# Seven block products in place of eight in 12 of 22 feed-forward pairs

## The chip, the cores and the metric

The kernel runs on one core of a Trainium2 chip. The metric is the device time of one execution in microseconds; several runs are given by their median.

## What is computed

Two layers act on 528 tokens (16 learned ones and a sequence of 512; the second layer hands out only the 512) of width 1024. A layer has four mixers that run side by side (a gated linear attention, a retention, a state-space branch, a gated delta rule), a gated sum of them, and a feed forward of hidden width 2816. The change is in the feed forward:

```python
    x = x + merged @ w_out
    h2 = rmsnorm(x, norm_ffn)
    gt, up = jnp.split(h2 @ w_gu, 2, axis=-1)
    return x + (jax.nn.silu(gt) * up) @ w_down
```

Everything is float32. The kernel reaches that precision on TensorE by splitting each operand into a high part (a cast to float32r) and a low part (the rest, value minus high part) and adding three products: high x high, high x low, low x high.

## The kernel before

Activations lie transposed, 128 channels on the partitions and the tokens in the free dimension. A weight panel of 128 output channels is 128 x 1024: eight blocks of 128 x 128, one for each k-block of the 1024 input channels. `wload` (line 180) brings a panel in two parts of four blocks: a DMA on SyncE's queue (L189, tile `wr`, 3 buffers), a cast on ScalarE to the high part (L190, tile `wh`, 5 buffers), a subtraction on VectorE for the low part (L192, tile `wl`, 5 buffers). `mmk` (L206) issues, for one k-block, the three products for each segment of tokens; `mm` does a panel, k-block by k-block, into one PSUM tile `pm` of two banks (2 buffers). Layer 0 has two segments of 264 tokens; layer 1 works on 512 tokens as one segment.

The 22 hidden panels of a feed forward come in three groups of 8, 7 and 7 (`FFG`). A pair is one gate panel and one up panel, of 128 hidden channels: two `mm` calls on the normalised activations `hh` and `hl`, then `silu2` (tanh on ScalarE, L365; (th + 1) x gate on VectorE, L366), the product with the up panel on VectorE (L1584), and the split of the result into `ah` and `al` (L199, L200). The factor of one half in the SiLU is put in afterwards. After each group `residual` multiplies the group's results by `w_down`, eight panels of 128 output channels, and adds to the residual stream `xs` on VectorE (L1545; the last two panels of the last group by halves of the tokens, L1555). The first pair of a layer goes by `head`, by halves of the tokens and mixed with the normalisation (`norm_sum`, `norm_finish`), whose own split is L199 and L200 on `hh` and `hl`.

The program orders TensorE's instructions by hand (`manual_schedule`); the other engines' order is set by the framework's scheduler, except that `after(ins)` puts the instructions traced within it behind `ins` on its engine. Side jobs are Python generators: `start` adds one, `pump` runs each by one step, `need` pumps until they are done. `mm` pumps once in four k-blocks.

One side job is `s5_prep` (line 1160): tables and matrices for the state-space branch, made from parameters alone, with many small VectorE operations (L1171), small matmuls (L1338), transposes (L1347) and DMAs to DRAM on GpSimd's and ScalarE's queues. Layer 0's runs beside the mixers of layer 0; layer 1's is started at the third pair of layer 0's feed forward and is needed at its end.

## Time and profile before

| | us |
|---|---|
| median of 3 runs | 2224.28 (2223.33 to 2229.99) |
| the profiled execution | 2226.7 |
| its span, first to last instruction | 2224.9 |
| TensorE busy | 2202.2 |
| VectorE busy | 1269.9 |
| ScalarE busy | 893.7 |

The span holds layer 0's mixers (to about 720 us), its feed forward (to about 1140), layer 1's mixers (to about 1835) and its feed forward (to about 2215). In the rows PE is TensorE's matmuls and PEld its weight loads, which run beside them; DVE is VectorE, ACT ScalarE, POOL GpSimd, SP SyncE. A matmul's duration runs from its start to its modelled end and overlaps the next one's, so the cost of one is the step from start to start. PEclk is the granted clock of TensorE as a share of 2.4 GHz.

### The profile page before, as it was taken

Reading aid. Unit: us, or ns where it says so; the run is one execution under the profiler, and the core shown is the slowest. Engines: PE = TensorE matmul, PEld = TensorE weight load, DVE = VectorE, ACT = ScalarE, POOL = GpSimd, SP = SyncE. Lnnn points to the kernel's source line nnn. Section 1 sums busy time; section 2 is a strip of 40 time slices with the busy share of each in tenths; the row PEclk is TensorE's granted clock in tenths of the full one; section 3 lists DMA queues with packets and bytes.
Section 4 is the critical chain, followed back from the end, with each engine's and each line's share of the span. In section 5 each row is a group of like instructions: output and inputs, shape, how many; then the busy total and the mean of one; then the engine's idle time right before and its main releaser. Section 6 shows DMA issues by size and latency. Waiting matters only on the chain. (4 is left out here: it accounts for less than half of the span.)

```text
span 2224.9 us, 41086 instructions
## 1 busy us (share of the span) xinstructions
PE 2202.2 (99%) x16300; PEld 2019.0 (91%) x16300; DVE 1269.9 (57%) x2505; ACT 893.7 (40%) x1920; POOL 189.5 (9%) x243
## 2 busy tenths in 40 slices
PE   9999999999999999999999999999999999999998
PEld 8999999999999999999999988787888888888887
DVE  7884566758444677533367844745385445434344
ACT  5653544433333433322346534644333334323232
POOL 2420021110000100000014121000000001000000
PEclk9999999999999999999999999999999999999999
DMA  4332222374233234332232332222643332332322
GB/s 129 104 105 66 86 77 77 111 228 141 89 91 119 96 110 124 124 87 94 88 119 83 106 95 83 75 72 72 202 122 90 95 123 91 90 100 91 98 93 83
DMA packets 144540, 229.73 MB, mean 103 GB/s; under 512 B 30044, under 2 KB 46884, under 8 KB 143836
## 3 DMA queue, kind: packets, MB, share of 16 engines
q1 hardware_dynamic: 136572, 208.98, 30.5%
q0 software_dynamic: 4032, 11.70, 1.6%
q10 hardware_dynamic: 3744, 6.42, 0.8%
q8 instruction: 128, 2.10, 0.4%
q14 instruction: 64, 0.52, 0.1%
HBM read 207.40 MB, written 19.65 MB: 102 GB/s over the span
## 5 line engine op out<-in xcount | busy, mean ns | idle before, releaser
L190 ACT CAST wh<-wr 128x512 fp32r<-128x512 f32 (+1 forms) x680 | 416.7, 614 | 1019.7 <-PE pm L206 841.7
L206 PE MATMUL pm<-hh,wh 128*128 128x264 f32 (+1 forms) x3120 | 799.6, 315 | 3.0 <-ACT hh L199 1.6
L206 PE MATMUL pm<-hl,wh 128*128 128x264 f32 (+1 forms) x3120 | 787.4, 312 | 5.6 <-POOL hl L200 2.9
L206 PE MATMUL pm<-hh,wl 128*128 128x264 f32 (+1 forms) x3120 | 783.2, 310 | 0.0
L192 DVE TENSOR_TENSOR wl<-wr,wh 128x512 fp32r<-128x512 f32 (+1 forms) x664 | 460.1, 695 | 537.3 <-ACT wh L190 528.3
L206 PEld LDWEIGHTS pm<-hh,wh 128*128 128x128 f32 x3120 | 513.5, 189 | 40.2 <-ACT hh L199 2.6
L206 PEld LDWEIGHTS pm<-hl,wh 128*128 128x128 f32 x3120 | 513.1, 189 | 38.9 <-POOL hl L200 4.4
L206 PEld LDWEIGHTS pm<-hh,wl 128*128 128x128 f32 x3120 | 512.8, 189 | 30.7
L206 PE MATMUL pm<-ah,wh 128*128 128x264 f32 (+2 forms) x542 | 146.0, 318 | 0.0
L206 PE MATMUL pm<-al,wh 128*128 128x264 f32 (+2 forms) x542 | 145.6, 317 | 0.0
L206 PE MATMUL pm<-ah,wl 128*128 128x264 f32 (+2 forms) x542 | 145.5, 317 | 0.0
L206 PE MATMUL pm<-bh,wh 128*128 128x264 f32 (+1 forms) x384 | 105.4, 328 | 0.8 <-DVE mg L445 0.5
L206 PE MATMUL pm<-bh,wl 128*128 128x264 f32 (+1 forms) x384 | 102.4, 321 | 0.0
L206 PE MATMUL pm<-bl,wh 128*128 128x264 f32 (+1 forms) x384 | 102.2, 320 | 0.0
L270 POOL TENSOR_TENSOR rs<-rs,mhalf 88x3 f32<-88x3 f32 (+1 forms) x10 | 8.4, 841 | 1060.1 <-ACT rs L269 1055.1
L206 PEld LDWEIGHTS pm<-ah,wh 128*128 128x128 f32 x542 | 91.4, 188 | 7.7 <-ACT wh L190 0.4
L206 PEld LDWEIGHTS pm<-al,wh 128*128 128x128 f32 x542 | 91.1, 188 | 7.2
L206 PEld LDWEIGHTS pm<-ah,wl 128*128 128x128 f32 x542 | 91.2, 188 | 6.9
L802 DVE SCALAR_TENSOR_TENSOR acc<-cvr,pk,acc 128x528 f32<-128x528 f32 x72 | 69.0, 960 | 8.8 <-ACT acc L799 7.9
L206 PEld LDWEIGHTS pm<-bh,wh 128*128 128x128 f32 x384 | 63.5, 188 | 8.1 <-DVE mg L445 1.3
L206 PEld LDWEIGHTS pm<-bh,wl 128*128 128x128 f32 x384 | 63.7, 188 | 5.4
L445 DVE SCALAR_TENSOR_TENSOR th<-th,pm 128x528 f32<-128x528 f32 (+1 forms) x48 | 33.3, 694 | 61.6 <-PE pm L206 55.4
(409 smaller groups left out, 2484.6 us busy)
## 6 DMA issues: line engine op xcount, KB each, us to landing
wr<-in_w_in SPq DMA_DIRECT2D x304, 256.0 KB, 2.7
wr<-in_w_gu SPq DMA_DIRECT2D x176, 256.0 KB, 2.6
wr<-in_w_br SPq DMA_DIRECT2D x64, 256.0 KB, 2.6
wr<-in_w_dn SPq DMA_DIRECT2D x64, 256.0 KB, 2.6
wr<-in_w_out SPq DMA_DIRECT2D x32, 256.0 KB, 2.6
wr<-in_w_dn SPq DMA_DIRECT2D x32, 192.0 KB, 2.4
s5mi<-s5m ACTq DMA_DIRECT2D x16, 256.0 KB, 3.1
mi<-s5mi SPq DMA_DIRECT2D x16, 256.0 KB, 3.7
```

Source lines behind the costliest of these rows:

```text
L190: i = nc.scalar.copy(hi[:, :n], raw[:, :n])
L192: j = eng.tensor_tensor(out=lo[:, :n], in0=raw[:, :n], in1=hi[:, :n].bitcast(F32), op=ALU.subtract)
L206: self.nc.tensor.matmul(ps[:m, i, :n], wt, x[k][:, t0:t0 + n], start=(k == 0 and i2 == 0), stop=(k == kt - 1 and i2 == 2))
L270: nc.gpsimd.tensor_tensor(out=dst, in0=dst, in1=self.mhalf[:dst.shape[0], :n], op=ALU.pow)
L445: nc.vector.scalar_tensor_tensor(out=self.sv(th, segs), in0=self.sv(th, segs), scalar=1.0, in1=br, op0=ALU.add, op1=ALU.mult)
L802: nc.vector.scalar_tensor_tensor(out=acc, in0=raw[:, w:w + T], scalar=conv[:, jt + w:jt + w + 1], in1=acc, op0=ALU.mult, op1=ALU.add)
```

## The change

In 12 pairs of each layer (`SEVEN`: the panels 4, 5, 7, 8, 10, 11, 13, 14, 16, 17, 19, 20) the two panels, the two halves of the 1024 input channels and the two halves of the tokens are seen as a product of 2 x 2 blocks and done with seven block products (Strassen's method in Winograd's form) in place of eight. `pair7` is such a pair. A product is 4 k-blocks x 3 terms = 12 matmuls over half of the tokens (264 in layer 0, 256 in layer 1). Three of its seven weight operands are panel halves as loaded, the other four (`s1` to `s4`) are sums and differences of such halves, made on VectorE (`comb`); each is then split as before. Three of the right-hand operands are blocks of `hh`, `hl` themselves, the other four are sums `T` of them, which `right_sums` makes once a layer beside pairs 1 to 3. Products add up in three PSUM tiles: `a` takes products 1, 3, 5 and 7 and is copied out on ScalarE after 1, 3 and 5 (`keep`); `c` takes 2 and 6, `d` takes 4. The four result blocks are put together in SBUF with `add`, and `finish` makes the SiLU product from them, in part by halves of the tokens.

The other pairs (`pair8`) keep their eight products, written as four units. `units` issues a list of units: the operands of a unit are traced four units before its products, behind the evictions of the three units before. `s5_prep` of layer 1 is started in layer 1's mixers, at the same place as layer 0's.

```diff
--- before.py
+++ after.py
@@ -54,6 +54,7 @@
     _o += _w
 NPK = _o
 FFG = [(0, 8), (8, 7), (15, 7)]
+SEVEN = [j for j in range(4, KF) if j % 3]
 
 
 def halves(segs):
@@ -1494,6 +1495,169 @@
         return bh, bl
 
 
+
+
+
+    def right_sums(self, segs):
+        nc = self.nc
+        (a0, n), (b0, _) = halves(segs)
+        t0 = a0
+        self.T = {}
+        rows = [self.f4(F32R, "xsum") for _ in range(2)]
+        for k in range(4):
+            top, low = self.f(name="xk"), self.f(name="xk")
+            for dst, kk in ((top, k), (low, k + 4)):
+                nc.vector.tensor_tensor(out=dst[:, t0:], in0=self.hh[kk][:, t0:].bitcast(F32),
+                                        in1=self.hl[kk][:, t0:].bitcast(F32), op=ALU.add)
+            b11, b12, b21, b22 = (x[:, c:c + n] for x in (top, low) for c in (a0, b0))
+            yield
+            for i in range(2):
+                t = self.f(name="xt")
+                x, y = t[:, 0:n], t[:, n:2 * n]
+                if i == 0:
+                    nc.vector.tensor_tensor(out=x, in0=b12, in1=b11, op=ALU.subtract)
+                    nc.vector.tensor_tensor(out=y, in0=b22, in1=x, op=ALU.subtract)
+                    nc.vector.tensor_tensor(out=b21, in0=b21, in1=y, op=ALU.subtract)
+                    sums = (1, 2)
+                else:
+                    nc.vector.tensor_tensor(out=x, in0=b22, in1=b12, op=ALU.subtract)
+                    nc.scalar.copy(y, b21)
+                    sums = (3, 4)
+                if i == 0:
+                    hi, lo = self.b(name="xsh"), self.b(name="xsl")
+                else:
+                    hi, lo = (r[:, k, :] for r in rows)
+                self.split(hi[:, :2 * n], lo[:, :2 * n], t[:, :2 * n])
+                for j, c in zip(sums, (0, n)):
+                    self.T[j, k] = (hi[:, c:c + n], lo[:, c:c + n])
+                yield
+
+    def pair7(self, srcs, segs, finish):
+        nc = self.nc
+        hs = halves(segs)
+        n = hs[0][1]
+        v = {}
+
+        def load():
+            for key, src, c in (("g0", 0, 0), ("u0", 1, 0), ("u1", 1, 512), ("g1", 0, 512)):
+                v[key] = self.ch("raw").rearrange("p a b -> p (a b)")
+                nc.sync.dma_start(v[key], srcs[src][:, c:c + 512])
+
+        def comb(key, x, y, op):
+            v[key] = self.ch("sum").rearrange("p a b -> p (a b)")
+            nc.vector.tensor_tensor(out=v[key], in0=v[x], in1=v[y], op=op)
+
+        def operands(key):
+            def run():
+                if key == "g0":
+                    load()
+                elif key == "s1":
+                    comb("s1", "u0", "u1", ALU.add)
+                elif key == "s2":
+                    comb("s2", "s1", "g0", ALU.subtract)
+                elif key == "s3":
+                    comb("s3", "g0", "u0", ALU.subtract)
+                elif key == "s4":
+                    comb("s4", "g1", "s2", ALU.subtract)
+                hi = self.wp.tile([P, 512], F32R, tag="wh", name="wh", bufs=5)
+                lo = self.wp.tile([P, 512], F32R, tag="wl", name="wl", bufs=5)
+                self.split(hi, lo, v[key])
+                v[key, 0], v[key, 1] = hi, lo
+            return run
+
+        def B(i, j):
+            s0 = hs[j][0]
+            return lambda k: (self.hh[4 * i + k][:, s0:s0 + n], self.hl[4 * i + k][:, s0:s0 + n])
+
+        def T(j):
+            return lambda k: self.T[j, k]
+
+        def products(key, to, x, first):
+            def run():
+                if key == "g0":
+                    v["a"] = self.psm()[:, 0, :n]
+                    for name in ("G", "U"):
+                        t = self.f(name=name)
+                        v[name, 0], v[name, 1] = (t[:, s0:s0 + n] for s0, _ in hs)
+                        v[name] = t
+                if first and to != "a":
+                    v[to] = self.psx([P, 512])[:, :n]
+                hi, lo = v[key, 0], v[key, 1]
+                for k in range(4):
+                    ks = slice(k * P, k * P + P)
+                    xh, xl = x(k)
+                    for i, (wt, xx) in enumerate(((hi, xh), (hi, xl), (lo, xh))):
+                        nc.tensor.matmul(v[to], wt[:, ks], xx, start=(first and k == 0 and i == 0),
+                                         stop=(k == 3 and i == 2), skip_group_check=True)
+            return run
+
+        def keep(dst, src):
+            return lambda: [nc.scalar.copy(v[dst], v[src]).ins]
+
+        def add(dst, src):
+            return lambda: [nc.vector.tensor_tensor(out=v[dst], in0=v[src], in1=v[dst], op=ALU.add).ins]
+
+        def rest():
+            return add(("G", 1), "c")() + add(("U", 1), ("U", 0))()
+
+        def last():
+            finish(v["G"], (v["a"], v["U", 1]))
+            return []
+
+        return [(operands("g0"), products("g0", "a", B(0, 0), True), keep(("G", 0), "a")),
+                (operands("s1"), products("s1", "c", T(1), True), keep(("U", 1), "c")),
+                (operands("s2"), products("s2", "a", T(2), False), keep(("G", 1), "a")),
+                (operands("g1"), products("g1", "d", B(1, 0), True), add(("G", 0), "d")),
+                (operands("s3"), products("s3", "a", T(3), False), keep(("U", 0), "a")),
+                (operands("s4"), products("s4", "c", B(1, 1), False), rest),
+                (operands("u1"), products("u1", "a", T(4), False), last)]
+
+    def pair8(self, srcs, segs, finish):
+        nc = self.nc
+        v = {}
+
+        def operands(i, h):
+            def run():
+                raw = self.wp.tile([P, 512], F32, tag="wr", name="wr", bufs=3)
+                hi = self.wp.tile([P, 512], F32R, tag="wh", name="wh", bufs=5)
+                lo = self.wp.tile([P, 512], F32R, tag="wl", name="wl", bufs=5)
+                nc.sync.dma_start(raw, srcs[i][:, 512 * h:512 * h + 512])
+                self.split(hi, lo, raw)
+                v[i, h] = lambda k: tuple(t[:, (k % 4) * P:(k % 4) * P + P] for t in (hi, lo))
+            return run
+
+        def products(i, h):
+            def run():
+                self.pump()
+                if h == 0:
+                    v[i] = self.psm()
+                for k in range(4 * h, 4 * h + 4):
+                    self.mmk(v[i], v[i, h], k, KD, self.hh, self.hl, segs)
+            return run
+
+        def last():
+            finish(self.pv(v[0], segs), self.pv(v[1], segs))
+            return []
+
+        return [(operands(i, h), products(i, h), last if i and h else lambda: []) for i in range(2) for h in range(2)]
+
+    def units(self, us, ahead=4):
+        made, pins = 0, []
+        for i, (_, products, then) in enumerate(us):
+            while made < min(i + ahead + 1, len(us)):
+                with self.after(*pins):
+                    us[made][0]()
+                made += 1
+            products()
+            pins = (pins + then())[-3:]
+
+
     def layer(self, l, xdram, segs, after):
         nc, a = self.nc, self.a
         t0 = segs[0][0]
@@ -1515,8 +1679,7 @@
         gst, gla = next(glap)
         ret = self.start(self.ret_gen(l, qk, rv))
         pst = {"go": False}
-        if l == 0:
-            prep = self.start(self.s5_prep(0, pst))
+        prep = self.start(self.s5_prep(l, pst))
         self.merge(l, 3, *parts, segs, "first")
         next(glap)
         self.need(ret)
@@ -1524,8 +1687,7 @@
         pst["go"] = True
         self.merge(l, 1, *self.head_finish(ret, rv, self.head_gates(l, C_RG, segs), self.par(l, "rtn"), segs), segs, "mid")
         sy = self.s5_proj(l)
-        if l == 0:
-            self.need(prep)
+        self.need(prep)
         self.need(gla)
         zh, zl = self.f4(F32R, "zh"), self.f4(F32R, "zl")
         s5 = self.s5_gens(l, sy, zh, zl, t0)
@@ -1564,31 +1726,43 @@
 
         residual([a["w_out"][l, j] for j in range(KD)], KD, self.mh, self.ml, xold, True)
 
-        prep = None
         for g0, gn in FFG:
-            ah, al = [], []
+            ah, al, act = [], [], [None, None]
+            us = []
             for j in range(gn):
-                if j % 4 == 0:
-                    h4, l4 = self.f4(F32R, "ah"), self.f4(F32R, "al")
                 srcs = [a["w_gu"][l, o + g0 + j] for o in (0, KF)]
-                sg = segs
+
+                def finish(pg, pu, j=j, sg=segs):
+                    if j % 4 == 0:
+                        act[:] = self.f4(F32R, "ah"), self.f4(F32R, "al")
+                    s = self.f(name="s")
+                    if len(pg.shape) == 3:
+                        self.silu2(s, pg, sg)
+                        nc.vector.tensor_tensor(out=self.sv(s, sg), in0=self.sv(s, sg), in1=pu, op=ALU.mult)
+                    else:
+                        nc.scalar.activation(s[:, t0:], pg[:, t0:], AF.Tanh, scale=0.5)
+                        nc.vector.scalar_tensor_tensor(out=s[:, t0:], in0=s[:, t0:], scalar=1.0, in1=pg[:, t0:],
+                                                       op0=ALU.add, op1=ALU.mult)
+                        for (s0, n), u in reversed(list(zip(halves(segs), pu))):
+                            nc.vector.tensor_tensor(out=s[:, s0:s0 + n], in0=s[:, s0:s0 + n], in1=u, op=ALU.mult)
+                    hv, lv = (t[:, j % 4, :] for t in act)
+                    self.split(hv[:, t0:], lv[:, t0:], s[:, t0:])
+                    ah.append(hv)
+                    al.append(lv)
+
                 if g0 + j == 0:
-                    sg = halves(segs)
-                    pg, pu = self.head(srcs, segs)
+                    finish(*self.head(srcs, segs), sg=halves(segs))
+                    sums = self.start(self.right_sums(segs))
                 else:
-                    pg, pu = (self.mm(self.wload(s, KD), KD, self.hh, self.hl, segs) for s in srcs)
-                if g0 + j == 2 and l + 1 < DEPTH:
-                    prep = self.start(self.s5_prep(l + 1, {"go": True}))
-                s = self.f(name="s")
-                self.silu2(s, pg, sg)
-                nc.vector.tensor_tensor(out=self.sv(s, sg), in0=self.sv(s, sg), in1=pu, op=ALU.mult)
-                hv, lv = h4[:, j % 4, :], l4[:, j % 4, :]
-                self.split(hv[:, t0:], lv[:, t0:], s[:, t0:])
-                ah.append(hv)
-                al.append(lv)
+                    us += (self.pair7 if g0 + j in SEVEN else self.pair8)(srcs, segs, finish)
+                if g0 + j == 3:
+                    self.units(us)
+                    us = []
+                    self.need(sums)
+            self.units(us)
             last = g0 + gn == KF
             if last:
-                self.need(prep)
                 self.norm_new(segs, xs, after(), then=KD if l + 1 < DEPTH else 0)
             residual([a["w_dn"][l, j, :, g0 * P:(g0 + gn) * P] for j in range(KD)], gn, ah, al, lambda j: xs[j], last)
         return xs
```

## Rows read from the trace of the kernel before

**Rows 1.** The page's parts 1, 2 and 5, the rows on TensorE.
```profile
PE 2202.2 (99%) x16300; PEld 2019.0 (91%) x16300; DVE 1269.9 (57%) x2505; ACT 893.7 (40%) x1920; POOL 189.5 (9%) x243
...
PEclk9999999999999999999999999999999999999999
...
L206 PEld LDWEIGHTS pm<-hh,wh 128*128 128x128 f32 x3120 | 513.5, 189 | 40.2 <-ACT hh L199 2.6
```

**Rows 2.** TensorE's waits (us in all, times, longest): 715 to 1140 us, 1830 to 2225 us.
```profile
PE pm L206 <- POOL hl L200: 1.4, 2, 0.8
...
PE pm L206 <- DVE hl L200: 0.4, 1, 0.4
...
PE pm L206 <- POOL hl L200: 1.5, 2, 1.0
...
PE px L320 <- POOL rs L270: 0.2, 1, 0.2
```

**Rows 3.** Busy time by engine in a window inside layer 0's third group.
```profile
core 0: us, PE busy (x) PEld busy (x) DVE busy (x) ACT busy (x) POOL busy (x), PEclk, DMA share, GB/s
1030.00:1076.00 46.00, 46.00 (x378) 46.00 (x377) 18.45 (x28) 14.50 (x24) 0.00 (x0) 1.00 0.28 92
```

**Rows 4.** Evictions of the up half in layer 1's second group: duration min/median/max, starts.
```profile
L1584 DVE TENSOR_TENSOR s<-s,pm x7: 686/687/689, 1990.5 to 2057.2; 128x512 f32<-128x512 f32 x7
```

**Rows 5.** Timeline of TensorE, layer 1, 256 columns: start, duration; 32 steps between.
```profile
1847.71 0.28 PE L206 MATMUL pm<-hl,wh 128*128 128x256 f32 x1
...
1851.48 0.28 PE L206 MATMUL pm<-hh,wh 128*128 128x256 f32 x1
```

**Rows 6.** VectorE by line and shape, layer 0, 1020 to 1076 us: count, busy us, mean ns.
```profile
L192 DVE TENSOR_TENSOR wl<-wr,wh 128x512 fp32r<-128x512 f32 x20 | 13.8, 691 | 26.5 <-ACT wh L190 26.5
...
L200 DVE TENSOR_TENSOR al<-s,ah 128x528 fp32r<-128x528 f32 x4 | 2.8, 709 | 0.4
```

**Rows 7.** VectorE by line and shape over the whole span, then two of its timeline.
```profile
L1171 DVE TENSOR_TENSOR s5t<-s5pw,rot 128x512 f32<-128x512 f32 x32 | 21.8, 685 | 0.1
L1472 DVE SCALAR_TENSOR_TENSOR sy<-s5w,sy 128x528 f32<-128x528 f32 x4 | 2.8, 701 | 0.7 <-ACT s5w L1471 0.7
L1555 DVE SCALAR_TENSOR_TENSOR x<-pm,x 128x264 f32<-128x264 f32 x4 | 1.7, 431 | 2.2 <-PE pm L206 2.2
...
876.98 0.69 DVE L192 TENSOR_TENSOR wl<-wr,wh 128x512 fp32r<-128x512 f32 x1 [2.04 <-ACT wh L190]
877.58 1.28 DVE L1171 TENSOR_TENSOR s5u<-s5pw,s5m 128x512 f32<-128x512 f32 x2
```

**Rows 8.** ScalarE by line and shape over the whole span.
```profile
L190 ACT CAST wh<-wr 128x512 fp32r<-128x512 f32 x648 | 400.2, 619 | 968.3 <-PE pm L206 797.3 <-issue 100.8 <-DMA wr<-in_w_in 48.0
L199 ACT CAST ah<-s 128x528 fp32r<-128x528 f32 x22 | 14.0, 635 | 9.3 <-DVE s L1584 9.3
L1360 ACT COPY u<-pm 128x264 f32<-128x264 f32 x16 | 5.3, 382 | 0.0
```

**Rows 9.** Timeline at an eviction of 256 columns in layer 1's last group.
```profile
2207.75 0.28 PE L206 MATMUL pm<-ah,wl 128*128 128x256 f32 x1
...
2208.07 0.42 DVE L1555 SCALAR_TENSOR_TENSOR x<-pm,x 128x256 f32<-128x256 f32 x1 [1.15 <-PE pm L206]
```

**Rows 10.** Loads of the feed forward's first weights: to landing, us min/median/max.
```profile
DMA to landing us min/median/max: 2.5/2.6/4.5
```

**Rows 11.** Busy time by engine, layer 0's mixers, then the same place in layer 1.
```profile
400.00:450.00 50.00, 50.00 (x547) 47.48 (x546) 39.60 (x94) 21.42 (x65) 5.58 (x7) 1.00 0.31 99
1480.00:1530.00 50.00, 50.00 (x429) 39.31 (x426) 30.05 (x79) 21.62 (x60) 2.01 (x2) 1.00 0.24 74
```

**Rows 12.** Busy time and granted clock ahead of layer 0's feed forward.
```profile
742.00:746.00 4.00, 2.65 (x18) 2.04 (x18) 3.84 (x9) 1.92 (x6) 1.40 (x2) 0.87 0.40 133
746.00:750.00 4.00, 3.79 (x18) 3.79 (x18) 2.34 (x4) 0.41 (x1) 0.87 (x2) 0.50 0.01 2
750.00:754.00 4.00, 4.00 (x28) 4.00 (x27) 3.75 (x10) 2.40 (x6) 1.60 (x2) 0.78 0.02 4
```

## Prediction

> **What bounds the kernel now.** The page's first part comes first: TensorE is busy for 99% of the span, VectorE for 57%, ScalarE for 40%, and TensorE's clock stands in the top tenth in every slice [rows 1]. A busy TensorE can still be a stretched one, so the second view is who TensorE waited for, taken over the two stretches that hold the feed-forward layers (715 to 1140 us in layer 0, 1830 to 2225 us in layer 1). The reader is to see the size, 0.2 to 1.5 us a row, three rows with 2.6 us and five with 3.3, and that they belong to the normalisation in front of a layer (`hh`, `hl`, `rs`) and the final sum, none to a weight operand or an eviction [rows 2]. So inside the pairs TensorE runs from matmul to matmul, and a pair costs what its matmuls cost.
>
> Third, the cost of one matmul, read from counts in a window and not from the duration column, because neighbouring matmuls overlap. With 264 columns: 378 in 46.00 us with TensorE busy throughout, 46.00/378 = 0.1217 us each [rows 3]. With 512 columns: seven evictions of layer 1's second group stand between 1990.5 and 2057.2 us, six pairs in 66.7 us, 11.12 us a pair of 48 matmuls, 0.2316 us each [rows 4]. With 256 columns, which the kernel has at the ends of layer 1's feed forward: the first start is 1847.71 us (the second matmul of the stretch, to leave out what a small matmul ahead of it stretched), the last 1851.48, 32 steps, 0.1178 us each [rows 5].
>
> **What the change removes on TensorE.** In layer 0 a pair is 2 outputs x 8 k-blocks x 3 terms x 2 segments = 96 matmuls of 264; as seven products of 4 k-blocks x 3 terms it is 84 of 264. Saved: 12 x 0.1217 = 1.46 us a pair, over 12 pairs 17.5 us. In layer 1 a pair is 48 of 512 and becomes 84 of 256: 11.12 - 84 x 0.1178 = 11.12 - 9.90 = 1.22 us, over 12 pairs 14.7 us. Together **32.2 us**, if TensorE never waits for anything new.
>
> Every one of the new matmuls has its own weights, and in layer 1 there are 75% more of them. The row says that this is paid for already: the 32 steps of 0.1178 us each took a weight load too. The Trainium skill ("TensorE: Matmul & The Clock Gate", Back-to-back issue gap) gives sustained spacings of about 81 ns at 128 columns and 131 ns at 512. An estimate for 256 between them is 98 ns, and by it layer 1's pair would go from 6.3 to 8.2 us, a loss of 1.9 us a pair; the trace has 232 and 118 ns there, so the measurement decides against it.
>
> **What it adds beside TensorE, per seven-product pair.** On VectorE: 7 subtractions for the low parts and 4 combinations, 11 of 128x512 at 0.69 us (L192 in this stretch, L1171) = 7.6 us; 3 adds of a half at 0.43 (L1555, which also reads PSUM) = 1.3; (th + 1) x gate 0.70 (L1472, both inputs in SBUF); 2 half products 0.86; the low part of the result 0.71 (L200): 11.15 us by durations [rows 6, 7]. Durations overlap when neither instruction needs the other: two took 1.28 us from a start that came 0.60 us after that of the one before [rows 7], so a step of 0.60 to 0.61 against 0.69. With 0.08 us off each of 18 instructions it is 9.7 us. The pair's TensorE time is 10.22 us in layer 0 and 9.90 in layer 1. **VectorE is therefore at 95 to 113% of a seven-product pair**, and at some 4 x 0.69 + 3 x 0.70 = 4.9 us of 11.7 in each ordinary pair. There are never more than two seven-product pairs in a row (4 and 5, 7, 8, 10 and 11, 13 and 14, 16 and 17, 19 and 20); over two of them and one ordinary pair VectorE needs 24 to 27 us of 31. Five buffers of operands let it be four products ahead, 4 x 1.4 = 5.6 us; converting an operand takes 0.62 + 0.69 us and may begin when a product ends, so some 4 us are left for VectorE to be late in, and two pairs in a row at worst use up 2 x (11.15 - 9.9) = 2.5. Operands: 0 on the path; without that lead 24 x about 1.1 = 26 us.
>
> On ScalarE: 7 casts x 0.62 + 4 evictions of a half at 0.38 + cast of the result 0.635 + tanh about the same = 7.1 us of 10 [rows 8]. Hidden as an amount. The order matters: the sum "a" is written by products 1, 3, 5 and 7, and each time ScalarE must copy it out while TensorE does just one other product. Available from the last matmul's start: 12 x 0.118 + 0.118 = 1.53 us in layer 1. Needed: the matmul's 0.28, 0.04 until an eviction began after such an end (2207.75 + 0.28, then 2208.07) [rows 9], the copy 0.38, and about 0.1 back: 0.80. One cast of 0.62 in front still fits (1.42); a cast and the 0.635 cast of the pair before do not (2.06), which costs about 0.5 us. At most one of the three turnarounds of a pair meets that, the first, where the result of the pair before is split. Bounds: 0 and 24 x 0.5 = 12 us. I take the middle, 6 us, since neither end has a nearer row: nothing in the trace shows a sum read out between two products.
>
> Loads: four of 256 KB a pair as before, but asked for together four products ahead. One lands in 2.6 us, at most 4.5 [rows 10]; the DMA engines are busy for 0.28 at 92 GB/s [rows 3], so 256 KB alone take about 0.8 us of all sixteen and the fourth is there 2.4 us after the first, while each is wanted a product (1.4 us) after the one before. 0, or 1 us in each of the 14 runs of such pairs if not covered.
>
> The sums of the right-hand blocks: per layer 4 x (2 x 0.70 + 4 x 0.43 + 2 x 0.70) = 18 us of VectorE in twelve steps beside pairs 1 to 3 (35 us in layer 0, 33 in layer 1), which hold 15 us of VectorE work otherwise. 0; the last sums are wanted two products into pair 4, so at worst 2 us a layer.
>
> The preparation for layer 1's state-space branch leaves layer 0's feed forward for layer 1's mixers. Its matmuls and transposes cost the same wherever they stand. Its instructions pass ScalarE, VectorE, GpSimd (the table DMAs) and ScalarE's DMA queue. Layer 0 already runs the same thing in that place: VectorE has 39.6 us of 50 there, and TensorE is busy for 50.00 of 50; layer 1 without it has 30.0 [rows 11]. 0; if the loop that waits for it ran dry, a few us once.
>
> The sum: 32.2 - 6 = 26.2. The profiled execution took 2226.7 us (span 2224.9 and 1.8 around it) against a median of 2224.3; so 2200.5 for a profiled one and **2198 us** for the median.
>
> **Rivals.** (1) *VectorE is the bound in the seven-product pairs.* For: 95 to 113% above, and its results depend on ScalarE's in between. Against: the lead, and the pair with 4.9 us in every three. If nothing is evened out the pair takes 11.15 us: 96 x 0.1217 - 11.15 = 0.5 saved in layer 0 and nothing in layer 1, 12 x 0.5 = 6 us: 2218. In between, half the loss: 2208. (2) *Slower: the turnaround of "a" lets TensorE idle and its clock falls.* The place: a run of seven-product pairs, when ScalarE's queue stands at the result's cast, which waits for a late VectorE, and the copy of "a" is behind it. For: in front of layer 0's feed forward this kernel shows the reaction: TensorE busy for 2.65 of 4 us, then a granted clock of 0.50 for 4 us (1.2 GHz) and 0.78 in the next 4 [rows 12]. The price there: 1.35 us idle and 4 x (0.13 + 0.50 + 0.22) = 3.4 us at the lower clock, 4.75. Once in each of 14 runs: 66 us, so 2224.3 - 32.2 + 66 = 2258. It decides from 32.2/14 = 2.3 us a run. Against: a wait for one copy is a part of 1.4 us, and a late VectorE catches up while TensorE waits. The Trainium skill says in "TensorE: Matmul & The Clock Gate" (Why this matters for your kernels) that idle TensorE stretches between bursts return it to half clock; the trace agrees, with 0.50 at 746 us. (3) *The narrow matmuls do not keep their spacing*, and the weight load paces them, 0.189 us by its duration [rows 1]: 84 x 0.189 = 15.9 us, +4.8 x 12 = 57 us in layer 1, and 2224.3 - 17.5 + 57 = 2264. The 32 steps with one load each speak against it. (4) *The saving isn't there*: the products wait for operands or buffers about as long as they save, 1.34 us a pair: 2224.
>
> **How the numbers follow.** Forecast 0.64 (2190 to 2207), rival 1 0.18 (2207 to 2218), rival 4 0.06, rival 2 0.11, rival 3 0.01. A measurement of this kernel tells about 0.3% (6.7 us) from no change. Faster needs under 2217.6: the forecast, nearly all of rival 1: 0.80. Same: 0.09. Slower: 0.11. The range starts at 2190 (no new wait, and 2 us of the slow clock that follows the norm gone) and goes to 2218, which leaves out rivals 2 to 4.
>
> **What the profile after would show.** TensorE at 98 to 99% with 16588 matmuls (-144 and +432); pairs of 10.2 to 10.6 and 9.9 to 10.3 us by the eviction rows; VectorE busy for 1270 + 24 x 6.3 + 36 = about 1460 us, ScalarE for 894 + 24 x 3.4 + 13 = about 990. Waits of TensorE for the copies of "a" should come to about 6 us. Wrong if: TensorE waits for low parts (rival 1); the granted clock falls inside the groups (rival 2); the starts of 256-column matmuls are further apart than 0.12 us (rival 3); layer 1's mixers lengthen (the moved preparation).

## The result, and the profile after

The kernel after takes **2200.98 us** (median of 4, 2199.85 to 2201.74) against 2226.81 us (median of 4, 2223.33 to 2229.99) for the kernel before: a ratio of 0.9884, with a 95% interval of 0.9865 to 0.9903, or 25.8 us less. The profiled execution took 2200.63 us, its span is 2198.9. Predicted were 2198 for the median and 2200.5 for a profiled execution, a saving of 26.2 us. (The forecast started from a median of 2224.28 for the kernel before; one more run beside the kernel after moved that median to 2226.81.) The total is right, but two of its terms are not, one too high and one too low, and the granted clock, which the sum left out, took some time as well. That these cancelled is luck.

The page's parts 1 and 2 after [rows 1]:

```profile
PE 2172.2 (99%) x16588; PEld 2013.5 (92%) x16588; DVE 1418.1 (64%) x2833; ACT 971.8 (44%) x2110; POOL 191.1 (9%) x243
...
PEclk9999999999999999999999999999999999999999
```

TensorE is the bound as before, with the 16588 matmuls that were foreseen. Its busy time fell by 30.0 us and the span by 26.0, so it stands idle for 4.0 us more. To see where, both traces are divided into stages at the evictions by halves of the tokens that end a layer's mixers and its feed forward (the line of [rows 7] with 128x264; in layer 0 the first of each four, in layer 1 the last): layer 0's mixers, its feed forward, layer 1's mixers, its feed forward. The columns are: stretch, its length, then busy time of each engine with the number of instructions, PEclk, share of the DMA engines, GB/s. First before, then after:

```profile
0.00:730.60 730.60, 725.77 (x6566) 708.86 (x6567) 468.91 (x990) 326.72 (x765) 90.63 (x123) 1.00 0.36 110
730.60:1135.00 404.40, 401.73 (x3299) 398.94 (x3299) 218.08 (x427) 133.55 (x241) 19.95 (x29) 0.99 0.34 106
1135.00:1840.20 705.20, 700.22 (x4734) 603.92 (x4733) 417.32 (x819) 316.83 (x709) 71.31 (x81) 1.00 0.33 101
1840.20:2214.20 374.00, 371.86 (x1689) 305.10 (x1689) 161.11 (x259) 114.78 (x200) 5.48 (x7) 1.00 0.29 89
```

```profile
0.00:732.70 732.70, 727.27 (x6566) 710.39 (x6567) 467.44 (x994) 326.70 (x765) 89.06 (x120) 1.00 0.36 112
732.70:1110.80 378.10, 375.52 (x3059) 374.00 (x3059) 242.71 (x423) 161.06 (x304) 6.99 (x8) 1.00 0.30 91
1110.80:1828.40 717.60, 709.36 (x4830) 610.58 (x4829) 467.90 (x988) 327.32 (x740) 87.41 (x105) 1.00 0.35 111
1828.40:2188.20 359.80, 357.43 (x2121) 316.36 (x2122) 235.68 (x420) 154.90 (x296) 5.49 (x7) 1.00 0.28 87
```

Read the lengths: +2.1, -26.3, +12.4, -14.2 us, in sum -26.0. Then length minus busy, TensorE's idle time: 4.83 to 5.43, 2.67 to 2.58, **4.98 to 8.24**, 2.14 to 2.37. The feed forwards gained next to no idle time (-0.09 and +0.23); layer 1's mixers, where only the preparation was added, gained 3.3 us. 96 matmuls went from layer 0's feed forward to layer 1's mixers with it.

TensorE's waits in the two feed forwards after, in the stretches that answer to [rows 2] (715 to 1115 and 1818 to 2199 us; us in all, times, longest):

```profile
PE pm L207 <- POOL hl L201: 1.5, 2, 0.9
PE pm L207 <- ACT hh L200: 0.7, 1, 0.7
PE pm L207 <- DVE hl L201: 0.3, 1, 0.3
...
PE pm L207 <- POOL hl L201: 1.5, 2, 1.0
PE pm L207 <- ACT hh L200: 0.8, 2, 0.6
...
PE px L321 <- POOL rs L271: 0.2, 1, 0.2
```

These are the waits of the normalisation that stood there before. Not one row has a weight operand (`wh`, `wl`) or a copy of a sum (L1599) as its releaser, the instruction whose end let TensorE go on.

Two windows inside runs of seven-product pairs, layer 0 and layer 1 (columns as above) [rows 3]:

```profile
911.00:927.00 16.00, 16.00 (x135) 16.00 (x134) 13.38 (x25) 9.76 (x20) 0.00 (x0) 1.00 0.10 25
1988.00:2004.00 16.00, 16.00 (x138) 16.00 (x137) 13.70 (x26) 9.87 (x21) 0.00 (x0) 1.00 0.12 38
```

TensorE is busy throughout. From the first to the last matmul that starts in the window there are 131 steps from 911.09 to 926.99 us, 0.1214 us each with 264 columns, and 134 from 1988.11 to 2003.95, 0.1182 us with 256; none is longer than 0.132. VectorE is busy for 84 and 86% there.

### The profile page after: what moved, and what is told of

It is laid out like the page before. It is cut to its first block, busy times and chain, and to the rows that moved or that the text cites. A ratio compares the mean times of both kernels' runs of the same rounds, so it can differ in the third digit from the quotient of the medians.

```text
span 2198.9 us, 42148 instructions
## 1 busy us (share of the span) xinstructions
PE 2172.2 (99%) x16588; PEld 2013.5 (92%) x16588; DVE 1418.1 (64%) x2833; ACT 971.8 (44%) x2110; POOL 191.1 (9%) x243
## 4 chain that ended last, share of the span: by engine, by line
PE 90%; DVE 4%; ACT 2%; issue 2%; DMA 1%; POOL 1%; DVEq 0%; SPq 0%; ACTq 0%; POOLq 0%
PE pm L207 69%; PE pm L1594 6%; PE px L1594 5%; DVE acc L803 1%; PE px L471 1%; DMA blkg<-dg 1%; PE px L1451 1%; PE px L1454 1%; DVE wl L193 1%; PE px L400 1%; PE px L477 0%; PE px L1080 0%; PE px L1413 0%; PE px L1104 0%; PE pm L836 0%
## 5 line engine op out<-in xcount | busy, mean ns | idle before, releaser
L207 PE MATMUL pm<-hh,wh 128*128 128x264 f32 (+1 forms) x2544 | 647.1, 315 | 2.8 <-ACT hh L200 1.5
L207 PE MATMUL pm<-hl,wh 128*128 128x264 f32 (+1 forms) x2544 | 633.7, 310 | 5.5 <-POOL hl L201 3.0
L207 PE MATMUL pm<-hh,wl 128*128 128x264 f32 (+1 forms) x2544 | 630.2, 308 | 0.0
L191 ACT CAST wh<-wr 128x512 fp32r<-128x512 f32 (+1 forms) x512 | 312.3, 612 | 684.0 <-PE pm L207 555.0
L193 DVE TENSOR_TENSOR wl<-wr,wh 128x512 fp32r<-128x512 f32 x496 | 340.4, 688 | 329.2 <-ACT wh L191 321.2
L207 PEld LDWEIGHTS pm<-hh,wh 128*128 128x128 f32 x2544 | 418.1, 189 | 31.3 <-issue 2.8
L207 PEld LDWEIGHTS pm<-hl,wh 128*128 128x128 f32 x2544 | 417.9, 189 | 29.8 <-POOL hl L201 4.6
L207 PEld LDWEIGHTS pm<-hh,wl 128*128 128x128 f32 x2544 | 417.6, 189 | 22.5
L200 ACT CAST wh<-sum 128x512 fp32r<-128x512 f32 x96 | 59.7, 622 | 96.1 <-PE pm L207 69.7
L201 DVE TENSOR_TENSOR wl<-sum,wh 128x512 fp32r<-128x512 f32 x96 | 65.1, 687 | 28.8 <-ACT wh L200 28.3
```

Source lines behind the costliest of these rows:

```text
L191: i = nc.scalar.copy(hi[:, :n], raw[:, :n])
L193: j = eng.tensor_tensor(out=lo[:, :n], in0=raw[:, :n], in1=hi[:, :n].bitcast(F32), op=ALU.subtract)
L200: return (nc.scalar.copy(hi, src), (eng or nc.vector).tensor_tensor(out=lo, in0=src, in1=hi.bitcast(F32), op=ALU.subtract))
L201: (eng or nc.vector).tensor_tensor(out=lo, in0=src, in1=hi.bitcast(F32), op=ALU.subtract))
L207: self.nc.tensor.matmul(ps[:m, i, :n], wt, x[k][:, t0:t0 + n], start=(k == 0 and i2 == 0), stop=(k == kt - 1 and i2 == 2))
```

## The experiments

**The preparation alone.** The kernel before, with only layer 1's preparation moved as the change moves it:

```diff
-        if l == 0:
-            prep = self.start(self.s5_prep(0, pst))
+        prep = self.start(self.s5_prep(l, pst))
...
-                if g0 + j == 2 and l + 1 < DEPTH:
-                    prep = self.start(self.s5_prep(l + 1, {"go": True}))
```

> The kernel before with one part of the change alone: the preparation of layer 1's state-space branch runs in layer 1's mixers, no seven-product pairs. The prediction put this move at 0, since layer 0 runs the same thing in that place with TensorE busy throughout: then the time stays that of before (ratio 1.000). The trace of the changed kernel speaks for a rival: TensorE waited for 3.9 us in layer 1's merge of the mixers against 0.8 us before, for VectorE and ScalarE; then the time rises by about 3 us (ratio 1.0015), with waits of 3 to 4 us between 1390 and 1420 us in the trace, and layer 0's feed forward is about 9 us shorter, layer 1's mixers about 12 us longer.

Measured: 2230.88 us against 2228.78, a ratio of 1.0010 (1.0001 to 1.0018), or +2.1 us (0.2 to 4.0). The interval only just leaves out no change. Layer 0's feed forward and layer 1's mixers, divided as above:

```profile
733.30:1129.80 396.50, 393.65 (x3203) 392.12 (x3203) 167.32 (x264) 119.40 (x208) 7.00 (x8) 1.00 0.30 92
1129.80:1846.10 716.30, 707.72 (x4830) 609.08 (x4829) 467.73 (x983) 327.60 (x740) 87.84 (x105) 1.00 0.35 108
```

The feed forward gives up 7.9 us, the mixers take 11.1, and their idle time is 8.58 us, as in the kernel after (8.24) and not as in the one before (4.98). So the 3.3 to 3.6 us of idle time come with the preparation, not with the seven products, and moving it costs 0.2 to 4.0 us where the prediction put 0.

The granted clock has a part in the 7.9 us. Behind the normalisation in front of layer 0's feed forward it fell in the kernel before, in this one and in the kernel after. Its cost is estimated here and below as the missing share of the clock times the length of the window. In the kernel before it was 4 x (0.13 + 0.50 + 0.22) = 3.4 us [rows 12], here 4 x (0.34 + 0.09) = 1.7:

```profile
749.00:753.00 4.00, 3.98 (x21) 3.77 (x22) 2.70 (x6) 0.52 (x2) 0.60 (x1) 0.66 0.02 4
753.00:757.00 4.00, 4.00 (x32) 4.00 (x31) 3.86 (x10) 2.35 (x7) 2.36 (x3) 0.91 0.00 0
```

and in the kernel after 1.7 as well:

```profile
748.00:752.00 4.00, 3.67 (x18) 3.67 (x19) 2.46 (x4) 0.41 (x1) 0.99 (x2) 0.57 0.00 0
```

So at equal clock the feed forward gives up 6.2 us and not 7.9, and between these two traces the move costs 11.1 - 6.2 = 4.9 us. For the seven products in layer 0 the kernel after and this one can be compared as they stand: 396.5 - 378.1 = 18.4 us.

**All 18 pairs.** Seven products in every pair from 4 on, so that no ordinary pair stands between them in which VectorE could catch up:

```diff
-SEVEN = [j for j in range(4, KF) if j % 3]
+SEVEN = list(range(4, KF))
```

> The changed kernel with all 18 pairs from the fifth on done by seven products (the six ordinary ones in between as well). It tells whether VectorE keeps up without an ordinary pair to catch up in, in runs of 4 and 7. If VectorE's step of 0.61 us counts (9.7 us of 9.9 to 10.2 a pair), the six pairs give 6 x (1.46 + 1.22) = 16 us more: 2185 us (ratio to before 0.981). If its durations count (11.15 us a pair), each run of seven falls behind by about 8 us, of which the lead covers 4: no gain over the change, about 2200 (0.988), with TensorE waiting for low parts.

Measured: 2181.14 us, ratio 0.9787 (0.9773 to 0.9800) to the kernel before. The feed forwards are 370.1 and 351.0 us long, 8.0 and 8.8 less than after. The clock differs here too. Behind the normalisation of layer 0 this trace lost 4 x (0.21 + 0.50 + 0.14) = 3.4 us to it, against 1.7 after:

```profile
744.00:748.00 4.00, 2.41 (x17) 2.12 (x16) 3.83 (x7) 1.50 (x5) 2.27 (x3) 0.79 0.26 86
748.00:752.00 4.00, 4.00 (x21) 4.00 (x20) 2.09 (x6) 0.83 (x3) 0.00 (x0) 0.50 0.02 4
752.00:756.00 4.00, 4.00 (x30) 4.00 (x30) 3.54 (x9) 2.03 (x6) 2.43 (x3) 0.86 0.00 0
```

Behind that of layer 1 it lost nothing (1.00 from 1812 to 1828 us), against 1.7 after (0.71 and 0.87 from 1832 to 1840 us). At equal clock the further six pairs save 9.7 and 7.1 us, 1.6 and 1.2 a pair, as the first twelve do (1.55 and 1.19, worked out below). A window in layer 1's last group, and its waits over layer 1's feed forward (1820 to 2178 us):

```profile
2062.00:2126.00 64.00, 64.00 (x545) 64.00 (x544) 61.89 (x115) 41.37 (x84) 0.00 (x0) 1.00 0.24 74
```

```profile
PE pm L207 <- POOL hl L201: 1.0, 1, 1.0
PE px L309 <- ACT sq L292: 0.7, 1, 0.7
```

VectorE is busy for 61.89 of 64 us, 97%, over 64/9.93 = 6.4 pairs in a row (9.6 us a pair), and TensorE waits for none of its results. So the price by start-to-start steps (9.7 us a pair) is the true one and the price by durations (11.15) is not: rival 1 falls. The rest of the gain over the kernel after, some 3 us, stands in layer 1's mixers (714.3 us against 717.6), whose code is the same: 1.7 of it is the lower clock that the trace of after has in them, shown further on, and 1.5 is idle time.

**The lead cut to two units.**

```diff
-    def units(self, us, ahead=4):
+    def units(self, us, ahead=2):
```

> The changed kernel with operands made two units ahead in place of four. If the lead is what covers VectorE's late stretches (finish of a pair: about 2 us of VectorE work at once), TensorE waits 0.5 to 1 us a pair for weights: 2201 + 12 to 24 us, 2213 to 2225. If VectorE keeps up unit by unit and the lead is spare, 2201 stays.

Measured: 2206.56 us, ratio 0.9897 (0.9883 to 0.9910); the feed forwards are 3.7 and 3.1 us longer than after, where 1.7 of the 3.7 us are the lower clock behind the normalisation (0.91, 0.50 and 0.74 from 742 to 754 us). Each has some 20 stretched steps. One of them, in the starts of TensorE's timeline in layer 1 (0.37 us from the first to the second, where 0.12 is usual):

```profile
1998.96 0.28 PE L1594 MATMUL px<-xsl,wh 128*128 128x256 f32 x1
1999.33 0.39 PE L1594 MATMUL px<-xsh,wl 128*128 128x256 f32 x1
```

Half the lead costs about 5 us by the stages, less than expected: VectorE keeps up unit by unit most of the time. The ratio's interval overlaps that of the kernel after, so the time alone does not show the loss.

**The turnaround without its cover.** Products 2 and 3 change places on TensorE, so that the sum `a` is copied out between two products that both write it:

```diff
+        def swapped():
+            products("s2", "a", T(2), False)()
+            products("s1", "c", T(1), True)()
...
-                (operands("s1"), products("s1", "c", T(1), True), keep(("U", 1), "c")),
-                (operands("s2"), products("s2", "a", T(2), False), keep(("G", 1), "a")),
+                (operands("s1"), lambda: None, lambda: []),
+                (operands("s2"), swapped, lambda: keep(("G", 1), "a")() + keep(("U", 1), "c")()),
```

> The changed kernel with products 2 and 3 exchanged on TensorE, so that the sum a, written by product 1, is written again with no product in between while ScalarE copies it out. It prices the turnaround that the prediction charged 6 us for. By the chain of 0.28 + 0.04 + 0.38 + 0.1 us TensorE waits 0.68 us at each of 24 pairs: +16 us over the changed kernel, 2217 us, and the granted clock stays at 1.0 if waits of that size do not trouble it. If it does trouble it (the slower rival), the pairs lengthen by several us each, over 2250 us. If the copy were not waited for at all: 2201.

Measured: 2217.00 us, ratio 0.9944 (0.9930 to 0.9957), some 15 us slower than after. The feed forwards are 9.9 and 8.8 us longer; 1.7 of the 9.9 us are again the lower clock behind the normalisation (0.93, 0.50 and 0.71 from 742 to 754 us), which leaves 17.0/24 = 0.71 us a pair. TensorE's longest row of waits, and one such place in the timeline of layer 1 (start, duration, and in brackets the idle time and its releaser):

```profile
PE pm L1594 <- ACT G L1599: 11.3, 24, 0.5
```

```profile
1888.72 0.28 PE L1594 MATMUL pm<-hh,wl 128*128 128x256 f32 x1
...
1889.04 0.37 ACT L1599 COPY G<-pm 128x256 f32<-128x256 f32 x1
...
1889.46 0.38 PE L1594 MATMUL pm<-xsh,wh 128*128 128x256 f32 x1 [0.46 <-ACT G L1599]
```

From the last matmul's start to the next write of `a` are 0.74 us; the prediction's chain had 0.80. The wait comes in every one of the 24 pairs once the copy has no product beside it. In the kernel after the copy starts 0.04 us (median of its 72) after the last matmul's end, 0.49 at most, and it is done at least 0.4 us before the next product writes `a`.

**The kernel after, again**, beside the next three:

> The changed kernel once more, beside the others of this call on the same chip, to set its gain against the parts. The parts by the traces so far: 17 to 18 us from layer 0's pairs, 13 to 14 from layer 1's, 2 to 3 lost by the moved preparation: 28 us, ratio 0.9875. The first comparison gave 0.9884; the prediction 0.988.

Measured: 2201.69 us against 2227.53, ratio 0.9880 (0.9867 to 0.9894). In layer 1's mixers, taken up to the first such eviction, TensorE idles for 9.36 us; in the first trace of the same kernel for 7.67. The longest wait there in the second trace is one that the first does not have. It belongs to the moved preparation:

```profile
PE px L1413 <- ACT s5e L1341: 3.2, 1, 3.2
```

A matmul of the state-space branch waits until ScalarE has copied a result of the preparation out of a PSUM tile that both use (`px`, L1341). On ScalarE that copy stood behind a cast of a weight panel, before which ScalarE had stood for 5.15 us until the panel's DMA landed:

```profile
1593.85 0.62 ACT L191 CAST wh<-wr 128x512 fp32r<-128x512 f32 x1 [5.15 <-DMA wr<-in_w_in]
...
1594.91 0.28 ACT L1341 COPY s5e<-px 128x128 f32<-128x128 f32 x1
```

So the moved work can make TensorE wait for a load of weights, in one execution and not in another.

**The preparation earlier.** All 18 pairs by seven, and layer 1's preparation started ahead of the attention's projections, where ScalarE has more room:

```diff
+        if l:
+            prep = self.start(self.s5_prep(l, pst))
         glap = self.gla_proj(l)
```

> All 18 pairs by seven products as in e2, and in layer 1 the preparation is started ahead of the projections of the gated linear attention in place of behind them, so that its table loads and first operations are over before that branch's own ones fill ScalarE. If the cost of the move (about 3 us) is that crowd, the waits for VectorE and ScalarE in layer 1's first merge fall back from 3 to 4 us to about 1, and the time falls by 2 to 3 us against e2: ratio to before about 0.9775. If the cost is the rest of the preparation, further on, it stays at 0.9787.

Measured: 2182.19 us, ratio 0.9796 (0.9783 to 0.9810), so no gain on 2181.14. TensorE's waits from 1100 to 1860 us:

```profile
PE pm L207 <- ACT ga L603: 3.3, 1, 3.3
...
PE pm L207 <- DVE mg L446: 0.5, 1, 0.5
```

The wait for `mg` shrank from 2.0 us to 0.5, and another on ScalarE, for `ga`, grew from 1.2 to 3.3.

**A nineteenth pair.** The same with pair 3 by seven too, the right-hand sums made beside pairs 1 and 2:

```diff
-SEVEN = list(range(4, KF))
+SEVEN = list(range(3, KF))
```

> As e5_prep_early, and the fourth pair by seven products too: the sums of the right-hand blocks are then made in pairs 1 and 2 (23 us), in which VectorE has 18 us for them and 10 us of its own. If the lead takes up what is late, one more pair in each layer gives 1.46 + 1.22 = 2.7 us, ratio 0.9763. If VectorE is too late there, TensorE waits up to 4 us a layer for the sums, and the time is that of e5_prep_early or up to 5 us more.

Measured: 2179.96 us, ratio 0.9793 (0.9776 to 0.9809). Against the 18 pairs (2181 to 2182) that can't be told from no change. By the stages the further pair does save: the feed forwards are 1.9 and 1.3 us shorter than in the trace of the 18 pairs, where the clock behind the normalisations cost the same. Layer 1's mixers are 3.6 us longer there, with the clock at 0.50 and 0.70 from 1364 to 1372 us. The sums of the right-hand blocks fit beside two pairs without a wait of their own.

**No lead to speak of**, one unit:

```diff
-    def units(self, us, ahead=4):
+    def units(self, us, ahead=1):
```

> The changed kernel with operands made one unit ahead in place of four. An operand then has one product of 1.4 us: copy of the sum a, cast, subtraction, about 0.4 + 0.6 + 0.7 = 1.7 us, and 2.4 where VectorE makes a sum first or a pair is finished. TensorE should wait 0.3 to 1 us at most of the 168 products: +70 to +150 us. It tells whether waits of that density bring the granted clock down (the slower rival of the prediction): if so, PEclk falls to 0.5 in places of the feed forward and the time exceeds before's by more than the waits alone; if not, PEclk stays at 1.0.

Measured: one execution, 2250.92 us, 24 and 26 us more than after in the two feed forwards. The two first rows of TensorE's waits, and a window in layer 1:

```profile
PE px L1594 <- DVE wl L201: 16.4, 34, 1.2
PE px L1594 <- ACT wh L200: 6.3, 24, 0.4
```

```profile
1900.00:1940.00 40.00, 37.71 (x244) 33.38 (x243) 25.09 (x45) 16.76 (x33) 0.00 (x0) 1.00 0.23 73
```

This is the slower kernel that rival 2 spoke of, but by another mechanism: some hundred steps a layer are stretched, by waits of up to 1.2 us; TensorE is busy for 37.71 of 40 us, and the granted clock stays at 1.00 in the pairs. The 50 us are the stretched steps alone. They show as idle time only in part (11 and 13 us of the 24 and 26): a matmul lasts 0.28 us and the next starts 0.12 us after it, so a step can grow by 0.16 before TensorE counts as idle. That the seven-product pairs of the kernel after have no step above 0.15 us says more than their idle time does.

**The preparation's first part back beside a feed forward.** All 18 pairs by seven; the exponentials, sines and first powers of layer 1's preparation run beside layer 0's feed forward, on a scratch tile of their own, and the rest waits until layer 1's mixers let it go:

```diff
-        scr = self.blk("s5t", [P, 2, 512])
+        scr = self.sp.tile([P, 2, 4 * SPAIR], F32, tag="s5s", name="s5s", bufs=1)
...
         while not st["go"]:
             yield
+        scr = self.blk("s5t", [P, 2, 512])
...
                     sums = self.start(self.right_sums(segs))
+                    if l == 0:
+                        self.pst = {"go": False}
+                        self.prep = self.start(self.s5_prep(1, self.pst))
```

> All 18 pairs by seven products as in e2, and of layer 1's preparation the first part (exponential, sine, the first powers, with the table loads) runs beside the first pairs of layer 0's feed forward, where ScalarE is idle for more than half of the time; only the rest runs in layer 1's mixers. If what the move costs is this first part meeting the gated linear attention's own table loads on ScalarE, the waits in layer 1's first merge fall from 3 to 4 us to about 1, without a new one in their place as in e5, and the time is 2 to 3 us under that of e2b_again. If the cost lies in the rest, the two are the same.

> All 18 pairs by seven products again (the kernel of e2), beside e8 on the same chip: ratio to before 0.979 as in e2.

Measured: 2181.83 us (ratio 0.9791, 0.9771 to 0.9810), and for the 18 pairs without it, beside it, 2181.30 (0.9788, 0.9768 to 0.9807): the same. TensorE's waits in the merge of layer 1 (1330 to 1420 us) with the first part moved:

```profile
PE pm L207 <- DVE mg L446: 0.5, 1, 0.5
PE pm L207 <- ACT ga L603: 0.3, 1, 0.3
```

That is what the kernel before has there, so the first part is what makes the merge wait. But the 2 us saved don't show in the time. At equal clock layer 1's mixers are 1.3 to 2.0 us shorter than in the two traces of the 18 pairs, and layer 0's feed forward, which now holds the first part, is about 1 us longer (here the clock stayed at 1.00 behind the normalisation of layer 0 and was 0.96 and 0.61 from 1118 to 1126 us); what is left is less than these times can tell.

## Why the prediction was right, and where its steps failed

**The saving of TensorE: right, a little small.** Foreseen were 17.5 us in layer 0 and 14.7 in layer 1; measured 18.4 (after against the preparation moved alone) and 14.2. In layer 0 the step was mis-sized: a count in a window also holds matmuls that start ahead of it. Of the 378 in [rows 3], 376 start inside, 0.1224 us apart and not 0.1217, and in the new pairs they are 0.1214 apart: 96 x 0.1224 - 84 x 0.1214 = 1.55 us a pair, 18.6 in all. In layer 1 it is 11.12 - 84 x 0.1182 = 1.19, 14.3 in all. The clock behind the normalisation cost 1.7 us in both traces of either comparison (in layer 1 it was 0.57 from 1844 to 1848 us before, 0.71 and 0.87 from 1832 to 1840 us after), so it does not enter. No run has the new order of units without the seven products, but the steps alone account for the whole saving. Rival 3 (narrow matmuls paced by their weight loads) is excluded by these steps. So is the slower result that the sustained spacing of the Trainium skill ("TensorE: Matmul & The Clock Gate", Back-to-back issue gap) would give.

**VectorE: right.** No pair waited for an operand. The experiment with all 18 pairs answers the question that the prediction left between 95 and 113%: it is 97%, and a lead of four units covers that even without a pair to catch up in. The busy time came to 1418 us and ScalarE's to 972, where about 1460 and 990 were foreseen: the sum for VectorE was made from durations, and busy time counts overlapping instructions once. The durations of its instructions sum up to 178 us more than before (187 foreseen), its busy time to 148 us more.

**The turnaround of `a`: wrong, 0 and not 6 us.** The chain was right (0.80 foreseen, 0.74 measured where it is bare), and so was the time available for it. The step that failed is the middle taken between 0 and 12 us on the thought that the result's cast meets the first copy: the copies start 0.49 us late at the most, and 0.4 us are left even in the worst turn. Both ends had been written down, and the end at 0 was the true one.

**The moved preparation: wrong, 2 to 5 us and not 0.** Foreseen was 0, because layer 0 runs the same thing in the same place without a wait, and "a few us once" if its cover were gone. The experiment with it alone measured +2.1 us (0.2 to 4.0), and between two traces, at equal clock, 4.9 us, of which 3.6 are idle time of TensorE. In all eight traces that have the preparation where the change puts it, TensorE idles for 6.2 to 9.4 us in layer 1's mixers up to the first such eviction and waits 2.0 or 2.1 us for `mg`, the gated sum of the merge; in the one trace of the kernel before it is 4.4 us, with 0.5 for `mg`. With the first part back beside the feed forward it is 5.1 us and 0.5. Part of the cost stands in the first merge of layer 1. TensorE's waits there after (1340 to 1440 us):

```profile
PE pm L207 <- DVE mg L446: 2.0, 3, 1.6
PE pm L207 <- ACT ga L603: 0.8, 1, 0.8
PE pm L207 <- ACT ex L675: 0.2, 1, 0.2
```

Before, `mg` had 0.5 and `ga` 0.3 us there and `ex` nothing. What was overlooked shows in two windows at the place of that merge, before and after:

```profile
1390.00:1406.00 16.00, 15.69 (x86) 12.83 (x85) 9.82 (x17) 15.70 (x22) 0.00 (x0) 1.00 0.22 66
```

```profile
1368.00:1384.00 16.00, 13.39 (x71) 10.56 (x70) 11.68 (x36) 15.83 (x23) 0.00 (x0) 1.00 0.23 66
```

ScalarE was busy for 15.70 of 16 us there already. The prediction looked at 1480 to 1530 us [rows 11], where ScalarE has 21.62 of 50, and not at the place that the moved work passes first. The other part differs from trace to trace. One is a wait for a DMA in layer 1's mixers (`xn<-dg`): 0.6 us before, 1.9 and 1.6 in the two traces of after, 1.7 with the preparation moved alone, 1.0, 0.4 and 0.3 in three traces with 18 pairs. Another is the wait of 3.2 us for the preparation's own copy, in the second trace of after. So the step that failed is the zero for this move; its size is known to within 2 to 5 us. Neither of the two ways of moving the preparation again brought the time below that of the 18 pairs alone. Which waits make up the rest is open.

**What cancelled.** Foreseen: 32.2 - 6 - 0 = 26.2. In the traces: 18.4 + 14.2 = 32.6, less 3.2 that moving the preparation alone costs in the same two stages (11.1 - 7.9), less 1.3 more in layer 1's mixers (12.4 against 11.1), less 2.1 in layer 0's mixers = 26.0. The last is not the change's: layer 0's mixers are the same code, and in the second trace of after they are 731.4 us long, not 732.7. In the first the granted clock was lower at the start. The window from 12 to 16 us, before and after (PEclk is the third column from the end):

```profile
12.00:16.00 4.00, 4.00 (x38) 4.00 (x37) 3.87 (x10) 2.88 (x8) 0.76 (x1) 1.00 0.29 61
```

```profile
12.00:16.00 4.00, 4.00 (x28) 4.00 (x27) 2.28 (x7) 2.45 (x7) 0.00 (x0) 0.71 0.43 86
```

The four us before that had 1.00 and 0.87, so the lower clock cost 4 x (0.13 + 0.29) = 1.7 of the 2.1 us. The 1.3 us in layer 1's mixers go with the clock too. After the wait of 1.7 us for the DMA there, it was lower:

```profile
1268.00:1272.00 4.00, 2.58 (x65) 2.26 (x66) 1.78 (x3) 2.84 (x5) 0.00 (x0) 0.81 0.49 149
1272.00:1276.00 4.00, 4.00 (x18) 2.79 (x16) 0.44 (x1) 1.07 (x2) 0.00 (x0) 0.77 0.17 57
```

That is again 4 x (0.19 + 0.23) = 1.7 us. The idle time of the stage is not larger than with the preparation moved alone (8.24 against 8.58). That kernel idled even longer at this place, in two waits, and its clock stayed at 1.00, in the next 4 us as well:

```profile
1288.00:1292.00 4.00, 2.32 (x68) 1.89 (x68) 2.61 (x3) 1.91 (x4) 0.76 (x1) 1.00 0.41 132
```

At equal clock the sum reads: 32.6 for the seven products, less 4.9 for the preparation, less 1.7 for the clock, which took 3.4 + 1.7 = 5.1 us from the kernel before and 4 x 1.7 = 6.8 from the kernel after, = 26.0. The 6 us charged for the turnaround, which costs nothing, stood in for 6.6 us of two things put at nothing. These figures are from one trace of either kernel; by the times the preparation costs less (2.1 us, at most 4.0), and that difference is not explained.

**The other rivals.** Rival 2 needed waits in the runs of seven-product pairs; there are none. Even where they were forced (a lead of one unit) its second half, the falling clock, did not come in the pairs. Rival 4 (nothing saved) is excluded by the stages. Of the zeros, the loads and the right-hand sums held: neither has a row among the waits of either feed forward.

**What the range was worth.** It was opened on the slow side for a bound by VectorE that the step of 0.60 us in [rows 7] spoke against. Had the step been trusted, 18 pairs rather than 12 would have looked affordable beforehand; that version takes 2181 us, 45 to 48 us below the kernel before and about 20 below the kernel after.

## What to carry to other kernels

When an engine is full, fewer matmuls are worth their start-to-start step times their count, and work added on another engine can be free: here it was, with VectorE at 97%, as long as the operands were made four products ahead. Count that engine by its steps, not by its durations. Give a sum that has to be read out between two products one product's time on another PSUM tile, and its turnaround may cost nothing, as here; without it, it was about 0.7 us each time. Work that a change moves aside is part of its price: look at the busy share of each engine in the very stretch that the moved work enters, not in a calmer one near it. Before two traces are compared stage by stage, compare their granted clock: here it moved a stage by 1.7 or 3.4 us without any change of code.

## What the runs showed of the hardware

A stream on VectorE ran at 97% for 64 us without delaying the engine that waits for its results. Some hundred short waits in a feed forward of 385 to 402 us, 1.2 us the longest, left TensorE's granted clock at 1.00 in its pairs, while one wait of 1.7 us for a DMA was followed by 0.77. Idle time of that size did not always have this effect: 1.68 us idle of 4 with the preparation moved alone left the clock at 1.00, and so did 1.60 of 4 behind the normalisation of layer 0 with the preparation started earlier (746 to 750 us), where the kernel before fell to 0.50 after 1.35 of 4 [rows 12]. What decides between the two is not shown by these runs. The prediction cited a section of the Trainium skill ("TensorE: Matmul & The Clock Gate", Why this matters for your kernels) by which idle stretches return TensorE to half clock; the falls agree with it, and the stretches that stayed at 1.00 show that idle time of this size need not do so.
